# The retention gate as seven half-size products, two heads' column sums a step later, and another order in the last head's steps and in the down weights' queue

## The chip, the cores and the metric

The kernel runs on one core of a Trainium2 chip. The metric is the device time of one execution in microseconds; for the kernel before, three runs are shown, and their median is what a change is held against. One further execution was taken by the hardware profiler; every row of a profile quoted here comes from it.

Engines are named as in the profile: PE is TensorE's matmul, PEld its weight load, DVE is VectorE, ACT is ScalarE, POOL is GpSimd, SP is SyncE, which here only issues DMAs.

## The reference

One layer of a decoder trunk on a prompt of 1024 tokens and 8 sampled tokens, model width 1024. The part around the change is the hybrid mixer: one input projection whose columns are split between four heads of differential attention and four heads of retention, with a swish gate on the retention heads.

```python
z = h @ w_in                      # h = rmsnorm(x), 1032 tokens x 1024; columns: qa ka va qr kr vr gr
oa  = diff_attention(qa, ka, va)  # two softmax maps a head, with a relative bias
o_r = retention(rotary(qr), rotary(kr) * scale, vr)      # chunks of 128 tokens, state S
a = head_rms(oa) * subln * (1 - lam_init)
r = head_rms(o_r) * silu(gr)      # the gate of this change: gr is h times a 1024 x 512 slice
x = x + concat(a, r) @ w_out
x = x + cross_attention(rmsnorm(x), memory)
x = x + square(relu(rmsnorm(x) @ w_up)) @ w_down         # hidden width 4096
```

All of it is in float32. A matrix product is done as three products of rounded halves (high by high, high by low, low by high), which the names `UH`, `UL` (activations) and `wh`, `wl` (weights) stand for.

## The kernel before, in words

**Stages.** (1) Queries and keys of retention, plain products. (2) Values of attention (`va`) and then of retention (`vr`): each 1024 x 1024 x 512 product is done by `token_block` as seven products of half size (512 x 512 x 256) with sums and differences of the operand's quarters, which stand ready in `XT`; the results are put together on DVE and ACT in four `acc` tiles. (3) Retention: a loop over eight chunks of 128 tokens. A chunk `t` does four transposes of queries and keys (`tr`), the scores (`sc`), the new state (`st`), the output (`op`, from the masked scores `Sm` and the state `S`), a norm for each head times the gate (`head_norm_gate`, which yields between the sums and the scaling), and four transposes of the result into an operand of the output projection (`to_operand`: `trR`, then `rh` on ACT, `rl` on DVE and two DMAs from POOL). Between these stand the 24 products of the gate for that chunk (`tokproj_parts`, tile `grp`) as plain products of 512 columns, three pieces of 9, 12 and 3 (`SEG` and the rest). (4) Attention: four heads, ten steps each, `g` from -4 to 39; beside each step's own work, products of the next head's queries and keys (`head_proj`, tile `qkp`) are put in as filler, `FILL` at a time; in the last head the filler is work for the output projection (`pr_half`) and the sampled tokens (`dsc`), in the order that `PLAN` has. `NORM_AT` says in which steps a finished head's column sums (`ct`), its factors and their row (`hrT`) are done. (5) Output projection, cross attention, the MLP's up product and then its down product (`dn`), the last two again as seven half-size products.

**What sets the order.** Tiles are placed by a pool allocator; a scheduler orders the instructions of each engine, except where `pin` keeps PE in the order of the program, and where `issue_after` and `behind` hold an instruction back behind another one. Each engine and each DMA queue then runs its instructions strictly in that order. SP issues nearly all loads, POOL issues the operand's stores. The down product's operands are loaded by SP too: `right_lower` fetches pieces `raw_h` of the hidden rows through a ring of three `raw` buffers, `load_left` the weights `raw_d` of a quarter `g`.

## Time and profile before

| | |
|---|---|
| three runs | 1474.23, 1470.69, 1475.36 us; median 1474.23 |
| the profiled execution | 1475.19 us, its span 1473.4 us |
| busy | PE 1455.7 us (99%), DVE 1107.9 (75%), ACT 679.7 (46%), POOL 314.4 (21%) |
| granted clock | 0.996 of full speed over the span |

The span starts with the first instruction; 1.8 us of the execution lie around it. A busy PE is one with a matmul in flight: matmuls are pipelined, one of 256 columns shows some 281 ns and the next starts 119 ns later, so that costs are read from the distance of starts. Groups of instructions are given as busy time and mean length; `[2.38 <-DVE c L2546]` behind a row says how long the engine had been idle before it and what ended that.

### The profile page before, as it was taken

To read this page: it belongs to the slowest core of one execution; us is meant where nothing else is said; L and a number is where in the kernel's file an instruction comes from. 1 tells how busy PE (TensorE), PEld (TensorE's weight loads), DVE (VectorE), ACT (ScalarE), POOL (GpSimd) and SP (SyncE) were. 2 spreads that over 40 slices of the span, in tenths; PEclk is the share of its full clock that TensorE was granted. 3 is DMA by queue.
4 is the path that set the end of the run, shared out by engine and by line. 5 is a ranking of instruction groups with operands and counts; after the bars stand their busy time and mean duration, and the time that the engine had idled before them with its cause. 6 is when DMAs were issued, how large, how long until landed. Compare 5 with 4: busy or idle time off the path is not lost.

```text
span 1473.4 us, 28129 instructions
## 1 busy us (share of the span) xinstructions
PE 1455.7 (99%) x11013; PEld 1401.0 (95%) x11013; DVE 1107.9 (75%) x2263; ACT 679.7 (46%) x1327; POOL 314.4 (21%) x345
## 2 busy tenths in 40 slices
PE   9999999999999999999999999999999999999998
PEld 7899779999889999999999999999999999999998
DVE  7666536888867756567868988888888878787876
ACT  7434435666552441267436533343435443343454
POOL 0035433122304511224122000000002211110380
PEclk9999999999999999999999999999999999999998
DMA  8155738215957265654762444333446764536273
GB/s 295 62 188 171 205 70 192 72 34 159 283 169 269 100 209 170 177 178 122 236 234 77 151 159 158 138 136 133 149 159 216 262 213 144 173 105 200 71 130 116
DMA packets 129833, 238.98 MB, mean 162 GB/s; under 512 B 13606, under 2 KB 80987, under 8 KB 129572
## 3 DMA queue, kind: packets, MB, share of 16 engines
q1 hardware_dynamic: 91354, 170.66, 36.0%
q0 software_dynamic: 27472, 46.93, 11.8%
q10 hardware_dynamic: 10874, 19.60, 3.5%
q8 instruction: 86, 1.41, 0.4%
q14 instruction: 47, 0.39, 0.1%
HBM read 171.13 MB, written 58.92 MB: 156 GB/s over the span
## 4 chain that ended last, share of the span: by engine, by line
PE 88%; DVE 5%; DMA 2%; ACT 2%; issue 1%; POOL 0%; ACTq 0%; SPq 0%; DVEq 0%
PE dn L2412 20%; PE Z L2244 9%; PE qkp L75 6%; PE Y L2244 6%; PE X L2244 6%; PE mq L75 6%; PE pr_m L75 6%; PE pr_o L75 5%; PE grp L75 3%; PE sp L75 2%; PE mv L75 2%; PE mk L75 1%; PE av L75 1%; PE mpv L75 1%; PE vap_z L524 1%; PE vrp_z L524 1%
## 5 line engine op out<-in xcount | busy, mean ns | idle before, releaser
L2412 PE MATMUL dn<-UH,wd 128*128 128x258 f32 (+1 forms) x1800 | 326.6, 283 | 3.0 <-DVE c L2546 3.0
L2412 PEld LDWEIGHTS dn<-UH,wd 128*128 128x128 f32 x1800 | 279.6, 190 | 3.6 <-ACT wd L2388 2.6
L2412 PE MATMUL dn<-UL,wd 128*128 128x258 f32 x900 | 254.6, 283 | 0.0
L2412 PEld LDWEIGHTS dn<-UL,wd 128*128 128x128 f32 x900 | 170.5, 189 | 0.1
L2546 DVE TENSOR_TENSOR c<-c,dn 128x258 f32<-128x258 f32 (+1 forms) x217 | 89.1, 417 | 38.5 <-PE dn L2412 35.8
L2270 ACT ACTIVATE hq<-r 128x258 f32<-128x258 f32 x128 | 53.7, 421 | 117.4 <-DVE r L2269 117.3
L2244 PE MATMUL Z<-T_h,wu 128*128 128x258 f32 x512 | 98.1, 283 | 0.0
L2244 PE MATMUL X<-UH,wu 128*128 128x258 f32 x512 | 97.5, 282 | 0.0
L2388 ACT CAST wd<-raw_d 128x512 fp32r<-128x512 f32 x96 | 58.7, 619 | 82.0 <-PE dn L2412 77.3
L2052 ACT CAST wu<-raw_up 128x512 fp32r<-128x512 f32 x96 | 59.0, 616 | 61.0 <-PE Z L2244 52.6
L2381 ACT CAST UH<-raw_h 128x1032 fp32r<-128x1032 f32 x56 | 58.7, 1055 | 55.2 <-PE dn L2412 27.9
L2244 PEld LDWEIGHTS X<-UH,wu 128*128 128x128 f32 x512 | 81.3, 188 | 0.0
L2244 PEld LDWEIGHTS Z<-T_h,wu 128*128 128x128 f32 x512 | 81.3, 189 | 0.0
L2382 DVE TENSOR_TENSOR UL<-raw_h,UH 128x1032 fp32r<-128x1032 f32 x56 | 72.9, 1301 | 9.9 <-ACT UH L2381 9.9
L2389 DVE TENSOR_TENSOR wd<-raw_d,wd 128x512 fp32r<-128x512 f32 x96 | 72.3, 759 | 10.2 <-ACT wd L2388 10.2
L2281 POOL DMA_DIRECT2D HT<-ht x32 | 17.2, 536 | 292.1 <-DVE ht L2280 291.6
L2244 PE MATMUL Z<-T_l,wu 128*128 128x258 f32 x256 | 72.3, 282 | 0.0
L2244 PE MATMUL X<-UL,wu 128*128 128x258 f32 x256 | 72.3, 282 | 0.0
L129 ACT CAST wh_u<-raw_u 128x1024 fp32r<-128x1024 f32 x43 | 44.7, 1047 | 57.6 <-PE mq L75 39.9
L2053 DVE TENSOR_TENSOR wu<-raw_up,wu 128x512 fp32r<-128x512 f32 x96 | 64.8, 689 | 3.6 <-ACT wu L2052 3.6
L2402 POOL TENSOR_TENSOR raw_d<-raw_d,raw_d 128x512 f32<-128x512 f32 x16 | 22.1, 1384 | 197.0 <-DVE raw_d L2398 145.3
L130 DVE TENSOR_TENSOR wl_u<-raw_u,wh_u 128x1024 fp32r<-128x1024 f32 x39 | 48.6, 1257 | 20.2 <-ACT wh_u L129 20.0
(616 smaller groups left out, 4707.4 us busy)
## 6 DMA issues: line engine op xcount, KB each, us to landing
raw_u<-in_wall SPq DMA_DIRECT2D x49, 512.0 KB
HT<-ht POOLq DMA_DIRECT2D x32, 516.0 KB, 3.0
raw_h<-HT SPq DMA_DIRECT2D x32, 516.0 KB
raw_up<-in_wall SPq DMA_DIRECT2D x32, 512.0 KB
raw_d<-in_wall SPq DMA_DIRECT2D x32, 512.0 KB
HQ<-hq ACTq DMA_DIRECT2D x32, 387.0 KB
raw_h<-HQ SPq DMA_DIRECT2D x24, 516.0 KB
cmk<-in_cmk SPq DMA_DIRECT2D x16, 512.0 KB
```

What stands on the lines that cost most here:

```text
L75: pinned(nc.tensor.matmul(out, l, r, start=start, stop=stop))
L130: (lo_engine or nc.vector).tensor_sub(wl[:, :n], raw[:, :n], wh[:, :n].bitcast(F32))
L2052: nc.scalar.copy(w[:, :512], src)
L2053: nc.vector.tensor_sub(w[:, 512:], src, w[:, :512].bitcast(F32))
L2244: pinned(nc.tensor.matmul(ps, l, r[:, k, :], start=first and k == 0 and x == 0, stop=k == 3 and x == 2, skip_group_check=True))
L2270: nc.scalar.activation(h[:, PLACE[quad], :], r, AF.Square)
L2381: nc.scalar.copy(h, rv)
L2382: nc.vector.tensor_sub(l, rv, h.bitcast(F32))
L2388: nc.scalar.copy(w[:, :512], src)
L2389: nc.vector.tensor_sub(w[:, 512:], src, w[:, :512].bitcast(F32))
L2412: pinned(nc.tensor.matmul(ps[:, part], l, r[:, k, cq], start=first and k == 0 and x == 0, stop=k == 3 and x == 2, skip_group_check=True))
L2546: nc.vector.tensor_add(y, y, ps)
```

## The change

- The gate is no longer a plain product inside the retention loop. It gets a `token_block` of its own (`ga`) between `va` and `vr`, with the swish in place of the plain scaling by the row factor. Its result goes to a DRAM buffer `gated` (issued from ACT's queue), and `fetch_gate` brings 128 rows of it back for each chunk (SP's queue). The rotations of queries and keys that stood in the `vr` block stand in the `ga` block.
- In the retention loop the filler is now the first 96 of the 144 products of head 0's queries and keys, 8 ahead of the loop and 6 and 5 in each chunk (`RFILL`). The transposes of chunk `t+1` are done in chunk `t` (`turn_step`), the scaling by the gate of chunk `t-1` after them, and `trR` of chunk `t-1` behind the output of chunk `t`.
- Behind the loop the operands of head 0 are split in two pieces of 344 columns where they were one of 688, with 36 fill products left ahead of the first scores.
- `NORM_AT` for the first two heads is moved by one step, `PLAN` of the last head has two `pr_half` steps earlier, the loading of a head's values and weights stands a step off, and the four loads of down weights of quarter 1 are held back until behind the last loads of quarter 0.

On PE the retention loop has no `grp` rows any more; chunk 1 is now 2 `sc`, 4 `st`, 4 `tr`, 6 `qkp`, 8 `op`, 4 `trR`, 5 `qkp`. On DVE, chunk 0's end and chunk 1 stood like this (`Sm`: masked scores, `S`: state, `gate`: the scaled output, `sn`: state of the sampled tokens, `UL`: a piece of the activations that is restored, `s`: the heads' sums):

```order
L768 COPY S_1630<-st_1608 128x128 x2
L146 SCALAR_TENSOR_TENSOR UL<-xagain_1560,g_mix,UH 128x512 x2
L140 TENSOR_SCALAR s_0_1643<-s_0_1643 128x4
L730 COPY kT_1672<-tr_1665 128x256
L665 SCALAR_TENSOR_TENSOR gate_1641<-op_1625,r_0_1644,gate_1641 128x128 x4
L741 TENSOR_TENSOR Sm_1687<-sc_1684,maskM 128x512
L770 SCALAR_TENSOR_TENSOR S_1726<-S_1630,rdec,st_1689 128x128 x2
```

and now:

```order
L140 TENSOR_SCALAR s_0_2105<-s_0_2105 128x4
L794 TENSOR_TENSOR Sm_2123<-sc_2120,maskM 128x512
L817 SCALAR_TENSOR_TENSOR S_2160<-S_2097,rdec,st_2125 128x128
L146 SCALAR_TENSOR_TENSOR UL<-xagain_2022,g_mix,UH 128x512 x2
L767 COPY kT_2137<-tr_2130 128x256
L704 SCALAR_TENSOR_TENSOR gate_2045<-op_2092,r_0_2106,gate_2045 128x128 x4
L644 TENSOR_TENSOR kraw_2056<-qkp_1_0_2058,rb 128x344
L817 SCALAR_TENSOR_TENSOR S_2160<-S_2097,rdec,st_2125 128x128
L715 TENSOR_TENSOR rl_2169<-trR_2163,rh_2168 128x512
L140 TENSOR_SCALAR s_1_2179<-s_1_2179 128x4
L747 SCALAR_TENSOR_TENSOR sn_2190<-so_2039,rdec,vb_2041 128x512 x2
L794 TENSOR_TENSOR Sm_2204<-sc_2201,maskM 128x512
```

The scaling by the gate of chunk 0 has moved behind the restored pieces, an eviction of the filler (`kraw`) has come in, and chunk 2's `Sm` stands behind the sampled tokens' `sn`. On POOL (`r`: the heads' factors, `vb`: products for the sampled tokens, `OPH`, `OPL`: the operand's stores) the same place was

```order
L141 TENSOR_TENSOR r_0_1644<-s_0_1643,half 128x4
L703 TENSOR_TENSOR vb_1661<-vb_1661,qkd 128x1024
L678 DMA OPH<-rh_1699 128x4x128
L678 DMA OPL<-rl_1700 128x4x128
L141 TENSOR_TENSOR r_1_1739<-s_1_1738,half 128x4
```

and is now

```order
L743 TENSOR_TENSOR vb_2041<-vb_2041,qkd 128x1024
L141 TENSOR_TENSOR r_0_2106<-s_0_2105,half 128x4
L717 DMA OPH<-rh_2168 128x4x128
L717 DMA OPL<-rl_2169 128x4x128
L141 TENSOR_TENSOR r_1_2180<-s_1_2179,half 128x4
L752 DMA out_state_s<-sn_2190 128x1024
```

so that the first `vb` stands ahead of the first `r`. On SP, in the down product's quarter 0, the loads from the seventh on stood as

```order
L2375 DMA raw_h_7_2_13922<-HT 128x4x258
L2361 DMA c_13488<-X_73 128x4x516
L2492 DMA raw_d_1_1_14439<-in_wall 128x1024
L2375 DMA raw_h_4_0_13927<-HT 128x4x258
...
L2375 DMA raw_h_5_2_14180<-HT 128x4x258
L2492 DMA raw_d_0_0_14436<-in_wall 128x1024
L2492 DMA raw_d_1_0_14438<-in_wall 128x1024
L2375 DMA raw_h_3_0_14184<-HQ 128x4x258
L2492 DMA raw_d_2_0_14440<-in_wall 128x1024
L2375 DMA raw_h_3_2_14188<-HQ 128x4x258
L2361 DMA c_13489<-X_73 128x516 x4
```

and now the weights of quarter 1 come last:

```order
L2379 DMA raw_h_7_2_14121<-HT 128x4x258
L2365 DMA c_13687<-X_73 128x4x516
L2379 DMA raw_h_4_0_14126<-HT 128x4x258
...
L2379 DMA raw_h_5_2_14379<-HT 128x4x258
L2379 DMA raw_h_3_0_14383<-HQ 128x4x258
L2379 DMA raw_h_3_2_14387<-HQ 128x4x258
L2365 DMA c_13688<-X_73 128x516 x4
L2496 DMA raw_d_0_0_14635<-in_wall 128x1024
L2496 DMA raw_d_0_1_14636<-in_wall 128x1024
```

Four weight loads that stood ahead of or between `raw_h_4` to `raw_h_3` now follow them.

The diff, cut to its core:

```diff
+    gated = dram.tile([T, 512], F32, tag="gated", name="gated")
...
-        def token_block(ready, nm, out_dec, fetch, between, after):
+        def token_block(ready, nm, out_dec, fetch, between, after, func=AF.Copy):
...
-                nc.scalar.activation(y[:, cs], y[:, cs], AF.Copy, scale=rstd1[:, t : t + 1])
+                nc.scalar.activation(y[:, cs], y[:, cs], func, scale=rstd1[:, t : t + 1])
...
+        def after_ga(q, acc):
+            if q in rot_ga:
+                rotate(rot_ga[q])
+            for t in {5: range(4), 3: range(4, 8)}.get(q, ()):
+                nc.scalar.dma_start(gated[t * P : t * P + P, :], acc[t // 2][:, t % 2, :])
...
-        op_vr = token_operands(U_TOK + 4, "vr")
-        token_block(op_va, "va", vdec[:8], rot_va, after_va, op_vr)
+        op_ga, op_vr = token_operands(U_TOK + 8, "ga"), token_operands(U_TOK + 4, "vr")
+        token_block(op_va, "va", vdec[:8], rot_va, after_va, op_ga)
+        token_block(op_ga, "ga", ga8[:8], rot_ga, after_ga, op_vr, AF.Silu)
...
+        filler = head_proj(0)
+        dec = decode_step(0)
+        next(dec)
+        gate = fetch_gate(0)
+        turned = turn_step(0)
+        fill(RFILL[0])
         for t in range(8):
+            qb, kT = turned
...
-            if pend:
-                pend()
-            for _ in range(SEG[1]):
-                next(grp)
+            if t < 7:
+                turned = turn_step(t + 1)
+            if scaled:
+                with behind("DVE"):
+                    next(scaled)
+            fill(RFILL[1])
...
-            nc.scalar.activation(gate, ps, AF.Silu, scale=rstd1[:, t : t + 1])
+            if pend:
+                pend()
+            fill(RFILL[2])
             scaled = head_norm_gate(op, gate, P, t, gate)
             next(scaled)
-            if t != 5:
-                next(scaled)
+            if t < 7:
+                gate = fetch_gate(t + 1)
...
-        fill(36)
-        to_operand(gate, P, 7, "7", ("ah", "al", 2))
-        until(0, 1, 0)
         load_stacks(0)
-        for _ in load_part(0, EARLY):
-            pass
+        for c in range(2):
+            for _ in load_part(0, slice(c * CH, c * CH + CH)):
+                pass
         filler = chain(filler, rest())
+        fill(28)
+        to_operand(gate, P, 7, "7", ("ah", "al", 2))
+        fill(6)
+        to_operand(lasts[0], 8, 8, "d", ("ah", "al", 2))
...
-            load_left((0, 1) if g == 0 else range(4))
+            with tc.issue_after(seen["SP"]) if g == 1 else nullcontext():
+                load_left((0, 1) if g == 0 else range(4))
...
-PLAN = ('dhh', 'ddhhd', 'hhdhhd', 'hhdhhd', 'hhdh', 'hhdh', 'hhd', 'hh', 'hh', '', '', '')
+PLAN = ('dhh', 'dhdhdhh', 'dhhd', 'hhdhhd', 'hhdh', 'hhdh', 'hhd', 'hh', 'hh', '', '', '')
-START = 36
+START = 2
-NORM_AT = (2, 3, 4, 5, 8), (2, 5, 6, 8, 9)
+NORM_AT = (2, 4, 5, 6, 8), (2, 5, 6, 8, 9)
-SEG = (3, 4, 0)
+RFILL = (8, 6, 5)
```

More of the change, by code (lines that the diff above doesn't have):

```diff
@@ L629, in decoder_step, with fill, until @@
+        def fill(n):
+            for _ in range(n):
+                next(filler, None)
+        def until(*key):
+            while key not in done:
+                next(filler)
         pin[0] = True
-        op_vr = token_operands(U_TOK + 4, "vr")
-        token_block(op_va, "va", vdec[:8], rot_va, after_va, op_vr)
+        op_ga, op_vr = token_operands(U_TOK + 8, "ga"), token_operands(U_TOK + 4, "vr")
+        token_block(op_va, "va", vdec[:8], rot_va, after_va, op_ga)
+        ga8 = A.tile([P, 512], F32, tag="t1", name="ga_8", bufs=1)
@@ L715, in decode_step, with turn_step @@
             yield
[L717 to L722 removed]
+        def turn_step(t):
+            tr = PS.tile([P, 512], F32, tag="tr", name=f"tr_{t}", bufs=2)
             for b in range(4):
@@ L771, in decoder_step @@
             S = Sn
+            if t == 5:
+                opd = PS.tile([P, 512], F32, tag="acc", name="opd", bufs=2)
+                for g in range(4):
+                    mm(opd[32 * g : 32 * g + 32, :], hsel, wvs[g // 2][:, 4 * (g % 2) : 4 * (g % 2) + 4, :], True, True)
+            if pend:
+                pend()
+            fill(RFILL[2])
+            scaled = head_norm_gate(op, gate, P, t, gate)
+            next(scaled)
+            pend = lambda gate=gate, t=t: to_operand(gate, P, t, f"{t}", ("rh", "rl", 1))
+            if t < 7:
+                gate = fetch_gate(t + 1)
             if t < 4:
@@ L1271, in rest @@
                 yield from head_proj(h)
-        filler = head_proj(0)
         decode = decode_steps()
-        def fill(n):
-            for _ in range(n):
-                next(filler, None)
-        def until(*key):
-            while key not in done:
-                next(filler)
-        pin[0] = True
-        fill(36)
-        to_operand(gate, P, 7, "7", ("ah", "al", 2))
-        until(0, 1, 0)
-        with behind("Activation", "DVE"):
-            head_units(1)
-        load_stacks(0)
-        for _ in load_part(0, EARLY):
-            pass
-        filler = chain(filler, rest())
+        pin[0] = True
+        load_stacks(0)
+        for c in range(2):
+            for _ in load_part(0, slice(c * CH, c * CH + CH)):
+                pass
+        with behind("Activation"):
+            nc.scalar.activation(A.tile([P, 1], F32, tag="pre", name="pre"), half[:, 0:1], AF.Exp)
+        filler = chain(filler, rest())
+        fill(28)
+        to_operand(gate, P, 7, "7", ("ah", "al", 2))
+        fill(6)
+        to_operand(lasts[0], 8, 8, "d", ("ah", "al", 2))
         par = operand_steps()
@@ L1372, in decoder_step @@
             if g >= 0:
-                if x == 0:
+                if x == 0 and h:
                     load_values(h)
-                    if h < 2:
+                if x == 1 and h < 2:
+                    with tc.issue_after(seen["ACT"]):
                         head_units(h + 2)
+            if g == -1:
+                with tc.issue_after(seen["ACT"]):
+                    load_values(0)
             if h < 3:
```

211 lines of the change are left out of this document (91 added, 120 removed).

## The prediction

> **What bounds the kernel now.** I read the page first, then PE's waits, then the chain of waits, then windows by stage. The page (engines' busy time and share; below it the shares of the chain that ended last):
>
> ```profile
> PE 1455.7 (99%) x11013; PEld 1401.0 (95%) x11013; DVE 1107.9 (75%) x2263; ACT 679.7 (46%) x1327; POOL 314.4 (21%) x345
> ...
> PE 88%; DVE 5%; DMA 2%; ACT 2%; issue 1%; POOL 0%; ACTq 0%; SPq 0%; DVEq 0%
> ```
>
> PE is the bound; only two things can shorten this: less PE work, or fewer of its stops. Its stops (who waited for whom: us in total, times, longest):
>
> ```profile
> PE dn L2412 <- DVE c L2546: 3.0, 2, 2.4
> PE trA L78 <- DVE e L1034: 2.1, 2, 1.4
> PE sp L75 <- DVE mn L1019: 1.8, 2, 1.0
> ...
> PE pr_half L75 <- DVE x_half L1356: 0.6, 1, 0.6
> ...
> PE hrT L78 <- DVE c L1086: 0.3, 1, 0.3
> PE vrp_x L524 <- ACT vr L532: 0.2, 1, 0.2
> ```
>
> The largest single stop, 2.4 us, lies in the down product; `trA`, `sp`, `pr_half` and `hrT` (4.8 us) lie in attention, where DVE is nearly full. Three windows (length, then busy us of PE, PEld, DVE, ACT, POOL, the granted clock, the DMA engines' share, GB/s): retention, what follows it, and the first head.
>
> ```profile
> 144.20:232.00 87.80, 87.60 (x517) 68.68 (x515) 40.86 (x103) 36.64 (x119) 31.13 (x33) 1.00 0.54 135
> 232.00:245.00 13.00, 12.92 (x84) 12.90 (x84) 5.11 (x13) 5.46 (x8) 6.38 (x9) 1.00 0.86 178
> 245.00:300.00 55.00, 54.15 (x363) 52.98 (x362) 49.59 (x131) 35.36 (x79) 7.64 (x20) 1.00 0.42 107
> ```
>
> In retention DVE works 47% of the time, then for 13 us 39%, then 90%: the gate's 512-column products are a wide cover for a thin chain. The change takes that cover away.
>
> **The change part by part.** *The products.* Rows of the chain (start, length, what):
>
> ```profile
> 106.04 5.97 PE vrp_x L524 x48
> 112.95 17.15 PE vrp_z L524 x144
> ...
> 157.87 2.78 PE grp L75 x12
> ...
> 173.12 3.71 PE grp L286 x16
> ...
> 234.68 9.44 PE qkp L75 x60
> ```
>
> A `grp` product of 512 columns costs 2.78/12 = 231.7 ns. There are 8 chunks x 24 = 192, or 44.5 us, and the sampled tokens' 16 in 3.71: 48.2 us go. The new block is the `vr` block's copy: 7 x 2 x 2 x 4 x 3 = 336 products of 256 columns at 17.15/144 = 119.1 ns, 40.0 us, and 4 x 4 x 2 = 32 small ones (the eight between the two rows above took 112.95 - 112.01 = 0.94, so 117 ns), 3.8. So 43.8 us come: **-4.4 us**. Its sums on DVE and ACT lie under its own products, as those of `va` and `vr` do. The 96 `qkp` products in the loop are moved, not added.
>
> One more change of blocks is added. The first eviction of a block needs the `acc` tile that the last block's stores still read; `vr` paid 0.2 us for it. Between nothing and twice this row: **+0.3**.
>
> *The down weights' queue.* The timeline around the 2.4 us stop (start, length, engine, line; in brackets the idle time before), two rows of the chain, and the clock's window:
>
> ```profile
> 1170.42 0.97 SPq L2492 DMA_DIRECT2D raw_d<-in_wall  x2
> 1174.51 0.38 SPq L2375 DMA_DIRECT2D raw_h<-HQ  x1
> 1174.93 0.51 SPq L2492 DMA_DIRECT2D raw_d<-in_wall  x1
> 1177.60 0.38 SPq L2375 DMA_DIRECT2D raw_h<-HQ  x1
> ...
> 1182.78 1.06 ACT L2381 CAST UH<-raw_h 128x1032 fp32r<-128x1032 f32 x1 [5.95 <-DMA raw_h<-HQ]
> ...
> 1186.55 1.23 DVE L2382 TENSOR_TENSOR UL<-raw_h,UH 128x1032 fp32r<-128x1032 f32 x1 [0.18 <-ACT UH L2381]
> ...
> 1188.26 0.36 PE L2412 MATMUL dn<-UH,wd 128*128 128x258 f32 x1 [2.38 <-DVE c L2546]
> ```
> ```profile
> 1163.76 3.88 DMA raw_h<-HT
> ...
> 1177.60 7.84 DMA raw_h<-HQ
> ```
> ```profile
> 1189.15:1192.56 3.41, 3.41 (x18) 3.41 (x17) 2.10 (x5) 0.00 (x0) 0.00 (x0) 0.50 1.05 378
> ```
>
> Two hidden pieces asked behind three weight loads take 1182.78 - 1174.51 = 8.3 and 7.84 us, where one asked alone took 3.88. So DVE reaches their split at 1186.55, the bank's eviction stands behind it, and PE stops for 2.38 us, then runs 3.41 us at half clock, worth 1.7. Without the three loads (1.57 MB, at this window's 378 GB/s 4.2 us) the pieces land some 4 us sooner and the split ends near 1183.6, 2 us ahead of PE. The held loads then follow at about 1180; their quarter starts only after 7 x 4 x 2 groups of 12 products, beyond 1210, so nothing is late next. From -4.1 (stop and slow clock) to 0 (the stop is only moved): **-4.0**.
>
> [...]
>
> *The retention steps.* Groups of that window (busy us, mean ns) and the order of a step:
>
> ```profile
> L741 DVE TENSOR_TENSOR Sm<-sc,maskM 128x512 f32<-128x512 f32 x8 | 5.5, 684 | 3.4 <-PE sc L75 3.4
> L676 DVE TENSOR_TENSOR rl<-trR,rh 128x512 fp32r<-128x512 f32 x7 | 4.8, 688 | 2.0 <-ACT rh L675 1.1 <-DMA OPL<-rl 0.9
> L770 DVE SCALAR_TENSOR_TENSOR S<-S,rdec,st 128x128 f32<-128x128 f32 x14 | 4.2, 340 | 0.0
> ...
> L730 DVE COPY kT<-tr 128x256 f32<-128x256 f32 x8 | 3.4, 423 | 2.1 <-ACT qblk L728 2.1
> L707 DVE SCALAR_TENSOR_TENSOR sn<-so,rdec,vb 128x512 f32<-128x512 f32 x4 | 3.0, 746 | 0.0
> L146 DVE SCALAR_TENSOR_TENSOR UL<-xagain,g_mix,UH 128x512 fp32r<-128x512 f32 x4 | 2.8, 749 | 0.7 <-ACT UH L145 0.7
> ```
> ```profile
> 156.03 1.13 DVE L665 SCALAR_TENSOR_TENSOR gate<-op,r,gate 128x128 f32<-128x128 f32 x4 [0.58 <-POOL r L141]
> ```
> ```profile
> L703 POOL TENSOR_TENSOR vb<-vb,qkd 128x1024 f32<-128x1024 f32 x2 | 3.8, 1887 | 0.0
> ```
>
> The window without `grp` (48.2) and without its 24 `qkp` at 9.44/60 = 157 ns (3.8) leaves 35.8 us for eight chunks, 4.5 each; with 11 fill products (1.7) a chunk lasts 6.2 us where it lasted 10. DVE's work in a chunk: `Sm` 0.7, `kT` 0.4, four `gate` 1.1, two `S` 0.7, `rl` 0.7 and small ones 0.2, 3.8 us; chunks 1 to 3 add 1.5 for two `UL` or two `sn`, and two of them 0.5 for the filler's eviction: up to 5.8 of 6.2. I laid out chunks 0 to 3 by hand from these lengths in the new order: in chunk 1 the two `UL`, `kT` and `gate` end about 1.0 us after PE wants `trR`; in chunk 2 `Sm`, behind two `sn`, is 0.2 late; in chunk 3 `gate` 0.9; in chunk 4 `Sm` 0.3; in chunk 6 `Sm`, behind a weight split, 1.0: 3.4 in all, each stop giving the next chunk slack. From 0.5 (the first chunk alone) to 8 (the rival below): **+2.5**.
>
> *Into the first head.* Behind the loop PE has 33 `qkp`, `trR`, 8 `qkp`, about 7.7 us, until the first scores. DVE must finish chunk 7 (`rl`, `gate` and an eviction behind `r`, some 5 us), then split the keys, and POOL must send eight copies, where the 13 us window above had DVE and POOL half free. From 0 to 3: **+1.0**.
>
> *Attention.* The column sums a step later free `hrT`'s 0.3; two `pr_half` steps earlier put 0.9 us of PE work ahead of scores that waited for DVE. Where DVE is the one that is late, moving filler moves the stop; from -4 (of the 4.8 nearly all gone) to +2: **-1.0**.
>
> Sum: -4.4 + 0.3 - 4.0 + 2.5 + 1.0 - 1.0 = **-5.6 us**. Against the profiled execution's own 1475.19 us this gives 1469.6; that execution lies 1 us above the median of 1474.23, so I say **1469.5**.
>
> **The rivals.** *All covered:* stops give slack, and DVE's 40.9 us, less what goes with `grp`, fit under some 51; then only the two savings stay, with -1 in attention: 1475.2 - 4.4 + 0.3 - 4.0 - 1.0 = 1466. For it: no engine but DVE is over 90% in a chunk. Against it: every engine runs in order, and the late ones stand ahead of the wanted ones.
>
> *The cover's loss eats the saving:* retention costs 5 and the head's start 3 instead of 2.5 and 1: 1474. For it the 90% of DVE in the window from 245; against it that there PE still lost only 0.85 us in 55.
>
> *The down product's stop stays or moves:* +4: 1473.5. Against it the margin of 2 us.
>
> *Slower:* the retention window's loads (size of each):
>
> ```profile
> brep<-brow SPq DMA_DIRECT2D x1, 2304.0 KB
> ...
> vb<-vrd SPq DMA_DIRECT2D x4, 256.0 KB
> xagain<-in_xT SPq DMA_DIRECT2D x2, 512.0 KB
> ```
>
> On POOL the first `vb` (1.9 us) now stands ahead of the first `r`, and it needs two of these loads, the second asked behind both `xagain`; `gate`, then `trR`, wait for that `r`. If they land some 11 us into the loop, PE stops 4.5 us in chunk 1, and in chunk 3, where two `vb` stand ahead of `r`, 2.4 more, each followed by 1.7 us of slow clock: +10.3 for the 2.5, 1477.5. It decides from a landing later than 7 us into the loop; with the head's start at 3 as well, 1479.5. For it: the DMA engines' share, 0.86 in the window behind retention; against it that `brep`, the largest load of this loop, now stands in the `vr` block.
>
> [...]
>
> That the change doesn't do what it says is excluded by the order: 208 `grp` products are gone, 368 of the block are there.
>
> **How the numbers follow.** My case 45% (1467 to 1472.5), all covered 22%, saving eaten 13%, stop stays 9%, slower 11%. A change is told from none here from 0.3%, 4.4 us: below 1469.8 is faster, above 1478.7 slower. Half of my case and nearly all of the covered one are faster: 0.48 with a little of the others; half of the slower case ends above 1478.7, with some room for what I haven't seen 0.09; the rest, 0.43, is the same. The range goes from 1463 (covered, attention at -4) to 1477, which leaves out most of the slower case.
>
> **What would show it.** `gap` rows in place of `grp`, some 44 us long; PE's start of retention 44 us later and its loop some 52 to 54 us long; PE waiting in it for `gate`, `Sm` or `r`, up to 1 us at a time; no half clock near the down product's start, and `raw_h` landing in 4 us there. Wrong: a PE stop over 2.4 us in retention, `vb` as what `r` waits for, a new wait for `raw_d`, or waits in attention that grew by more than 2 us.

## The result, and the profile after

| | before | changed |
|---|---|---|
| runs | 1472.90 us median of 8 (1470.58 to 1475.36) | 1482.01 us median of 8 (1477.90 to 1482.88) |
| profiled execution, its span | 1475.19, 1473.4 us | 1482.29, 1480.5 us |

The changed kernel is slower: 1.0052 of the time before, interval 1.0041 to 1.0063, where 1469.5 us, 0.3% less than the 1474.23 of the kernel before, was forecast and 1477 was the upper end of the range. Its runs fall into two groups, three at 1478 to 1479 and five at 1482 to 1483; what parts them is the clock, below.

The page after the change (engines' busy time; shares of the chain that ended last) and PE's waits (who waited for whom: us in total, times, longest):

```profile
PE 1458.4 (99%) x11173; PEld 1410.6 (95%) x11173; DVE 1123.6 (76%) x2284; ACT 684.2 (46%) x1341; POOL 317.7 (21%) x349
...
PE 83%; DVE 7%; DMA 3%; issue 2%; ACT 2%; POOL 1%; SPq 0%; DVEq 0%; ACTq 0%; POOLq 0%
```
```profile
PE sp L75 <- DVE mn L1025: 4.6, 6, 2.8
PE trA L78 <- DVE e L1040: 3.0, 4, 1.6
PE av L75 <- DVE al L1059: 1.4, 1, 1.4
...
PE dn L2416 <- DVE c L2551: 0.9, 2, 0.6
```

The stop in the down product is gone (3.0 to 0.9 us), but `sp`, `trA` and `av`, all in attention, now wait 9.0 us where they waited 4.2 (0.3 of it `av`). To see where the time went, the program was cut at the same instructions in both traces: the first product of the added or the `vr` block, the first transpose of retention (the sampled tokens' `tr_d`), the first score, the last half product, and the first product of `mq` (cross attention), of the up and of the down product. Windows (length, then busy us of PE, PEld, DVE, ACT, POOL, the granted clock, the DMA engines' share, GB/s), first before, then after; the after has one row more, for the added block:

```profile
99.00:143.30 44.30, 44.08 (x371) 43.14 (x369) 30.28 (x36) 17.71 (x26) 26.73 (x17) 1.00 0.56 191
143.30:249.60 106.30, 106.01 (x638) 87.06 (x638) 51.06 (x119) 43.62 (x130) 37.51 (x42) 1.00 0.61 144
249.60:444.70 195.10, 189.92 (x1375) 179.97 (x1375) 159.18 (x426) 116.64 (x250) 40.47 (x75) 1.00 0.51 147
...
1133.80:1473.40 339.60, 330.54 (x2742) 329.60 (x2740) 268.36 (x445) 146.13 (x242) 79.95 (x74) 0.98 0.53 159
```
```profile
99.40:143.10 43.70, 43.70 (x370) 43.16 (x369) 31.42 (x36) 16.01 (x24) 26.12 (x16) 1.00 0.59 196
143.10:186.80 43.70, 43.70 (x370) 43.06 (x368) 21.05 (x23) 15.64 (x24) 1.31 (x3) 1.00 0.45 153
186.80:245.00 58.20, 57.53 (x429) 50.53 (x429) 41.78 (x108) 31.85 (x116) 32.10 (x34) 1.00 0.86 201
245.00:453.50 208.50, 197.91 (x1376) 183.92 (x1375) 164.84 (x436) 117.55 (x254) 47.15 (x87) 0.98 0.53 144
...
1144.00:1480.50 336.50, 329.73 (x2742) 328.56 (x2740) 269.30 (x445) 146.40 (x242) 79.84 (x74) 0.99 0.54 160
```

The two blocks take 87.4 us for 44.3 (+43.1). Retention up to the first score takes 58.2 for 106.3 (-48.1), for the same PE work less the 208 `grp` products. Together that is **-5.0**, all that the products could give. Then attention, with the same PE work (1376 matmul records for 1375), takes 208.5 for 195.1: **+13.4**. The down product gives -3.1, the stages between them +1.4, the start +0.4; the sum is the 7.1 us between the spans. So the question is attention. Cut at every 48th of its 192 score products: 39.7, 44.1, 44.9, 34.1 us (to the last of them) and a rest of 32.4 us before; 43.8, 49.4, 47.0, 36.5 and 31.8 after.

The largest of its stops is this one; the timeline after (start, length, engine, line; in brackets the idle time before and what ended it):

```profile
388.04 0.27 PE L78 MATMUL hrT<-ident,c 128*8 128x128 f32 x1 [0.23 <-DVE c L1106]
...
391.93 0.33 SPq L1116 DMA_DIRECT2D rbh<-hrow  x1
...
398.10 1.29 DVE L1143 TENSOR_TENSOR oraw<-oraw,rbh 128x512 f32<-128x512 f32 x2 [1.89 <-DMA rbh<-hrow]
...
400.12 0.41 PE L75 MATMUL sp<-KA,Q 128*128 128x320 f32 x1 [2.77 <-DVE mn L1025]
```

and this is the same place before:

```profile
376.44 0.27 PE L78 MATMUL hrT<-ident,c 128*8 128x128 f32 x1
...
379.96 0.32 SPq L1110 DMA_DIRECT2D rbh<-hrow  x1
...
385.80 0.69 DVE L1137 TENSOR_TENSOR oraw<-oraw,rbh 128x512 f32<-128x512 f32 x1 [0.47 <-DMA rbh<-hrow]
```

A finished head's factors go through `hrT` to DRAM and come back as a row over all partitions, `rbh`, 9.4 us later before (376.44 to 385.80) and 10.1 us later after (388.04 to 398.10). `NORM_AT` moved the sums, the factors and `hrT` by a step, but not its last entry, the step in which DVE multiplies by the row (8 in both). DVE reaches that instruction, waits 1.89 us for the row, and the score evictions behind it wait too; PE stops for 2.77 us. The row is made in two DMAs on SP's queue: the second, `rbh`, is asked 3.5 us (before) and 3.9 us (after) behind `hrT` and lands 5.8 and 6.2 us later.

The second place, after the change and, in the second block, before:

```profile
326.86 0.39 PE L75 MATMUL av<-al,VH 128*128 128x256 f32 x1 [1.38 <-DVE al L1059]
...
328.36 2.97 PE L75 MATMUL ct<-ones,sq 128*128 128x1 f32 x16
```
```profile
322.74 1.84 PE L75 MATMUL ct<-ones,sq 128*128 128x1 f32 x16
```

Before, the 16 records of `ct` stood ahead of that weighing (`av`), and PE had them to do while DVE made `al`. They now come behind it. The windows there, and behind the 2.77 us stop:

```profile
325.42:328.83 3.41, 2.03 (x16) 1.97 (x16) 3.32 (x5) 1.25 (x2) 0.31 (x2) 1.00 0.32 61
328.83:332.24 3.41, 3.41 (x17) 3.41 (x17) 0.85 (x5) 0.00 (x0) 0.42 (x1) 0.50 0.00 0
332.24:335.66 3.42, 3.42 (x16) 3.36 (x15) 0.69 (x1) 0.58 (x1) 1.24 (x1) 0.50 0.00 0
...
400.51:403.93 3.42, 3.42 (x27) 2.71 (x25) 3.42 (x12) 1.15 (x4) 0.00 (x0) 0.50 1.18 389
```

Each stop is followed by half clock, 6.83 and 3.41 us of it. There `av` products of 256 columns start 213 or 214 ns apart, 120 just ahead of it, and the records of `ct` 213 for 112: some 4.6 us lost, by an estimate from these distances. In the second window PE is busy all the time, with `ct`, and yet a third one at half clock follows.

### The profile page after: what moved, and what is told of

Same layout as the page of the kernel before. It is cut to its first block, busy times and chain, and to the rows that moved or that the text cites. A ratio compares the mean times of both kernels' runs of the same rounds, so it can differ in the third digit from the quotient of the medians.

```text
span 1480.5 us, 28578 instructions
## 1 busy us (share of the span) xinstructions
PE 1458.4 (99%) x11173; PEld 1410.6 (95%) x11173; DVE 1123.6 (76%) x2284; ACT 684.2 (46%) x1341; POOL 317.7 (21%) x349
## 4 chain that ended last, share of the span: by engine, by line
PE 83%; DVE 7%; DMA 3%; issue 2%; ACT 2%; POOL 1%; SPq 0%; DVEq 0%; ACTq 0%; POOLq 0%
PE dn L2416 20%; PE Z L2248 9%; PE Y L2248 6%; PE mq L75 6%; PE pr_m L75 6%; PE X L2248 6%; PE qkp L75 5%; PE pr_o L75 2%; PE mv L75 2%; PE mk L75 1%; PE av L75 1%; PE mpv L75 1%; PE vap_z L507 1%; PE gap_z L507 1%; PE vrp_z L507 1%
## 5 line engine op out<-in xcount | busy, mean ns | idle before, releaser
L2393 DVE TENSOR_TENSOR wd<-raw_d,wd 128x512 fp32r<-128x512 f32 x96 | 70.2, 738 | 10.8 <-ACT wd L2392 10.7
L1031 ACT ACTIVATE e<-e,mn 128x128 f32<-128x128 f32 (+6 forms) x64 | 49.7, 777 | 33.0 <-DVE mn L1025 32.4
L75 PE MATMUL qkp<-UH,wh_u 128*128 128x344 f32 x192 | 63.8, 332 | 0.3 <-DVE gate L704 0.3
```

Of the source, the lines that this page charges most:

```text
L75: pinned(nc.tensor.matmul(out, l, r, start=start, stop=stop))
L1031: nc.scalar.activation(e[:, :n], e[:, :n], AF.Exp, bias=mn[:, m : m + 1], scale=-1.0, accum_out=sm[:, m, q : q + 1])
L2393: nc.vector.tensor_sub(w[:, 512:], src, w[:, :512].bitcast(F32))
```

## The experiments

Medians in us; the ratio is to the runs of the kernel before on the same chip (their medians 1473.65, 1473.84, 1473.59 and 1473.88 in the four groups). "Lost to the clock" is the mean span times one less the mean granted clock; the last column is the mean span without it. That takes half clock for half the pace, where by the distances above it is 1.8 to 1.9 times as slow, so that the loss is a little high. In all 17 profiles the last 4.7 to 9.1 us of the span are at half clock, while PE's last product ends 5.7 to 6.1 us before the span does: 2.4 to 4.6 us of what each of these executions "lost" lie there, most of it with no product left to slow, so that only differences between the rows count.

| run | median (runs) | ratio and interval | lost to the clock | rest |
|---|---|---|---|---|
| before (all its runs of the first two groups) | 1473.8 (46) | | 4.6 | 1467.6 |
| changed | 1482.0 (8) | 1.0052 (1.0041 to 1.0063) | 6.7 | 1472.4 |
| a_norm: sums as before | 1479.8 (5) | 1.0035 (1.0021 to 1.0049) | 7.1 | 1470.3 |
| a_plan: last head's order as before | 1480.8 (5) | 1.0056 (1.0042 to 1.0069) | 8.3 | 1471.5 |
| a_out9: the row's reader a step later too | 1480.7 (5) | 1.0048 (1.0034 to 1.0062) | 6.8 | 1472.2 |
| b_norm: before, sums a step later | 1477.6 (10) | 1.0025 (1.0016 to 1.0035) | 7.1 | 1468.9 |
| b_down: before, down weights held back | 1474.1 (12) | 1.0006 (0.9997 to 1.0014) | 4.5 | 1468.1 |
| n_nodown: sums as before, weights not held | 1478.1 (8) | 1.0026 (1.0016 to 1.0036) | 6.6 | 1469.5 |
| n_rfill: sums as before, 16 fill moved | 1476.0 (11) | 1.0018 (1.0009 to 1.0026) | 5.8 | 1468.5 |
| n_ct: sums as before, `ct` in pairs | 1478.8 (11) | 1.0029 (1.0016 to 1.0042) | 5.8 | 1471.0 |
| b_ct3: before, `ct` three times | 1488.9 (4) | 1.0103 (1.0089 to 1.0118) | 11.9 | 1474.9 |
| n_rfill2: sums as before, 32 fill moved | 1481.6 (5) | 1.0056 (1.0043 to 1.0069) | 10.4 | 1468.7 |
| n_vals: n_rfill, values loaded as before | 1478.8 (6) | 1.0035 (1.0022 to 1.0048) | 6.9 | 1470.7 |
| n_rfill2v: both of the last two | 1482.0 (6) | 1.0052 (1.0040 to 1.0064) | 6.9 | 1473.0 |
| a_rfill: changed, 16 fill moved | 1479.4 (6) | 1.0048 (1.0034 to 1.0063) | 7.1 | 1470.8 |
| n_plan: n_rfill, last head's order as before | 1476.1 (11) | 1.0016 (1.0006 to 1.0026) | 5.9 | 1468.5 |
| n_chunk: n_plan, 24 fill moved | 1476.8 (11) | 1.0022 (1.0011 to 1.0033) | 5.6 | 1469.4 |

### The column sums a step later

```diff
 # a_norm: the changed kernel; b_norm makes the opposite edit in the kernel before
-NORM_AT = (2, 4, 5, 6, 8), (2, 5, 6, 8, 9)
+NORM_AT = (2, 3, 4, 5, 8), (2, 5, 6, 8, 9)
```

> The changed kernel with only the column-sum steps put back (NORM_AT's first row 2, 3, 4, 5, 8 as before; all else as changed). Theory A: the sums a step later cost about 8 us in attention in two ways. The eight ct products of head 0 no longer stand ahead of the weighing that waits for al (a PE stop of 1.38 us near 326, then 6.83 us at half clock), and the gain row leaves one step later while its reader (oraw<-oraw,rbh on DVE) stays, so DVE waits for the row (0.61 us near 349, 1.89 us near 396) with score evictions queued behind it (PE stops of 1.6 and 2.77 us, then 3.41 us at half clock). Then this run takes 7 to 9 us less than the changed kernel, about 1474, the span's clock is 0.997 or more, and the three places show no PE stop over 1 us. Rival B: DVE carries work into attention that the thinner retention no longer hides, and stops wherever it is full; then this run gains at most 2 us and the stops only move.

> The kernel before with only the column sums a step later (NORM_AT's first row 2, 4, 5, 6, 8). Theory A: it is slower than the kernel before by 5 to 9 us though retention is untouched, with a PE stop at al<-trA near 329 us and a DVE wait for rbh near 394 us. Rival B (the thinner retention is the cause): within 1.5 us of the kernel before.

In the kernel before, where nothing else was touched, the edit costs 3.7 us (2.4 to 5.2; theory A had 5 to 9). Its trace has the predicted wait, and the stop, in the kernel with the old retention:

```profile
393.51 1.29 DVE L1137 TENSOR_TENSOR oraw<-oraw,rbh 128x512 f32<-128x512 f32 x2 [2.30 <-DMA rbh<-hrow]
...
395.53 0.63 PE L75 MATMUL sp<-KA,Q 128*128 128x320 f32 x1 [3.09 <-DVE mn L1019]
```

followed by 6.83 us at half clock. The stop at `al` did not come in it. In the changed kernel, undoing the edit takes the stop at `al` away and brings the other two down to 0.73 and 0.87 us, but gains only 2.2 us, not 7 to 9, and the intervals of the two versions overlap: a stop of 0.64 us at `ct`, which waits for `sq` on ACT, comes in place of the one at `al`, and that profile has half clock there too and at two more places. So theory A has the mechanism right and about doubles its size; rival B as put (at most 2 us, stops only move) is excluded by b_norm, though about half of the loss is left for it.

```diff
 # a_out9: the changed kernel
-NORM_AT = (2, 4, 5, 6, 8), (2, 5, 6, 8, 9)
+NORM_AT = (2, 4, 5, 6, 9), (2, 5, 6, 8, 9)
```

> The changed kernel with the reader of the gain row a step later as well (NORM_AT's first row 2, 4, 5, 6, 9 in place of 2, 4, 5, 6, 8). Theory A: DVE no longer waits for the row, so the stops near 355 and 397 us (1.6 and 2.77 us) and the half clock behind the second go, some 4 to 5 us; the stop near 326 us stays, since the ct products are still late there. Rival B (DVE is simply full): no gain over 1 us. Rival C (the order in the last head): the stop near 397 us stays.

DVE now waits 0.57 us for the row instead of 1.89, but the two products by `rbh` then stand ahead of another thing that PE wants:

```profile
393.75 0.69 DVE L1143 TENSOR_TENSOR oraw<-oraw,rbh 128x512 f32<-128x512 f32 x1 [0.57 <-DMA rbh<-hrow]
...
399.44 0.42 PE L75 MATMUL pr_half<-UH,wh_u 128*128 128x344 f32 x1 [3.62 <-DVE x_half L1354]
```

The stop moved and grew, and the median stayed within 1.3 us. Not all of the 3.62 us is the row's: one product `e` in front of that eviction takes 1.80 us, where 0.75 is usual (below, the cover of the first head). The expectation of 4 to 5 us is missed: the place of the waits changed and their sum did not fall, 10.2 us of PE's stops in attention as changed and 10.8 here.

### The last head's order

```diff
 # a_plan: the changed kernel
-PLAN = ('dhh', 'dhdhdhh', 'dhhd', 'hhdhhd', 'hhdh', 'hhdh', 'hhd', 'hh', 'hh', '', '', '')
+PLAN = ('dhh', 'ddhhd', 'hhdhhd', 'hhdhhd', 'hhdh', 'hhdh', 'hhd', 'hh', 'hh', '', '', '')
```

> The changed kernel with only the last head's order put back (PLAN as before; all else as changed). Theory A (the sums a step later are the cause): the time stays within 1.5 us of the changed kernel, and the stops near 326, 355 and 397 us stay. Rival C (the other order of the decode and half steps costs the time after 384 us): 2 to 3 us less than the changed kernel, and the 2.77 us stop near 397 goes.

1.2 us less, with five runs spread over 3.4 us; the stops of 1.40, 1.60 and 2.54 us stay where they were. n_plan, with eleven runs beside n_rfill's eleven (below), has 1476.1 against 1476.0, and 1468.5 in both without the loss to the clock. Rival C's 2 to 3 us are out; whatever the order is worth lies within some 2 us of nothing. (n_plan's stretch from score 144 to the last half product is 2.7 us longer than n_rfill's, where 0.5 was allowed; two half-clock windows, 3.4 us, fall into it.)

### The down weights' queue

```diff
 # b_down: the kernel before; n_nodown undoes it in a_norm
-            load_left((0, 1) if g == 0 else range(4))
+            with tc.issue_after(seen["SP"]) if g == 1 else nullcontext():
+                load_left((0, 1) if g == 0 else range(4))
```

> The kernel before with only the down weights' loads held back (the one line at load_left; all else as before). As predicted, the 2.38 us stop and the half clock at the down product's start are gone, raw_h lands in about 4 us, and the time falls by 3 to 4 us. Rival: the stop is not there in every execution (the run with only the sums moved, which has the old queue, showed 0.61 us there and no half clock), so the median falls by 1 us or less.

> The changed kernel with the column sums as before and the down weights' loads not held back. As predicted for the queue: a PE stop of 2.4 us and a half clock return at the down product's start, and the time is 3 to 4 us above the run with the sums as before. Rival (the stop comes only in some executions): within 1.5 us of it.

Nothing: 1.0006 (0.9997 to 1.0014), that is from 0.4 us less to 2.1 more, and n_nodown is not slower than a_norm. Not that the edit fails: with it `raw_h` is not asked behind `raw_d`, and the wait for it is shorter (b_down: asked at 1175.92, split begun at 1181.02). But the old queue does not always make PE stop that long. In b_norm, which has it:

```profile
1182.30 0.38 SPq L2375 DMA_DIRECT2D raw_h<-HQ  x1
...
1188.76 1.05 ACT L2381 CAST UH<-raw_h 128x1032 fp32r<-128x1032 f32 x1 [4.04 <-DMA raw_h<-HQ]
```

6.5 us from the request to the split (6.2 in n_nodown) where the profile before had 8.3, with the same order on the queue. PE's stops there are 0.60 us, and 0.42 in n_nodown. In b_ct3 (below), the fourth profile with the old queue, the split begins 6.4 us after the request and PE stops for 1.29 us. Half clock follows only in the profile before. So 1.1 us or more of the 2.38 us stop, and its half clock, are what that one execution had; what made its load land 2 us later than the same request in the other three is open. The edit is not free of stops either: b_down's profile has two of 0.66 and 0.58 us, at 1203.9 and 1211.9.

### The cover of the first head

```diff
 # n_rfill: a_norm with 16 qkp out of the loop (a_rfill: the same two edits in the changed kernel)
-RFILL = (8, 6, 5)
+RFILL = (8, 5, 4)
...
         load_stacks(0)
+        fill(16)
         for c in range(2):
```

> The changed kernel with the column sums as before and 16 of the first head's qkp moved out of the retention loop (RFILL 8, 5, 4 in place of 8, 6, 5), to stand between the loop and the first key splits. Theory D: the first head is slow (43.8 us from the first score to the 49th against 39.7 before) because DVE comes out of the loop with chunk 7's work and the key splits in hand; 2.5 us more of pure PE work there let it catch up, so that stretch shrinks by 1.5 to 2.5 us while the loop, which has hardly a stop, does not grow by it. Rival E: the loop was just covered; it then stops 2 us more, and nothing is gained.

> The changed kernel with only 16 qkp moved from the retention loop to before the first key splits; the column sums stay a step later. So far: changed 1482.0, with the sums as before 1478.1 to 1479.8, with both 1476.0. If the parts add, this run is at 1478.5 to 1480, its first stretch at 42.0 us, and the DVE wait for rbh near 394 us and the PE stop behind it stay. If the sums a step later cost nothing by themselves and all was carried DVE work, it is at 1476 like the run with both.

As theory D has it: the stretch of the first 48 scores falls from 43.8 to 42.0 us, and the loop stays (58.2 us from its first transpose to the first score, a_norm 57.7). The run is the best of the changed family, 1476.0. With a_rfill the four corners are 1482.0 as changed, 1479.4 with the fill moved, 1478.1 to 1479.8 with the sums as before, 1476.0 with both: the parts add within a microsecond, though with five to eleven runs each no such difference is known to better than some 2 us. The first two rows are that stretch before and as changed; the two behind them are from n_rfill, the loop and the stretch:

```profile
249.60:289.30 39.70, 38.85 (x258) 37.80 (x258) 36.03 (x99) 26.82 (x58) 5.39 (x14) 1.00 0.38 106
```
```profile
245.00:288.80 43.80, 41.11 (x258) 37.49 (x257) 39.90 (x109) 27.24 (x62) 13.67 (x25) 1.00 0.55 126
```
```profile
187.00:245.10 58.10, 57.63 (x429) 50.37 (x430) 43.14 (x112) 32.02 (x116) 33.91 (x37) 1.00 0.89 206
245.10:287.10 42.00, 40.10 (x258) 37.56 (x258) 38.09 (x105) 27.29 (x62) 11.90 (x22) 1.00 0.56 124
```

PE has the same 258 products in each. What differs is DVE's work: 36.03 us in 39.7 before, 39.90 in 43.8 as changed, 38.09 in 42.0 here, 37.52 in 40.9 in n_rfill2. It is 91 or 92% of the stretch in these four, and DVE's idle time stays between 3.4 and 3.9 us: the stretch grows and shrinks by what DVE's work does. What came ahead of the first score before is now done here. By their lengths (which overlap a little) the splits of keys and queries are 2.05 us of it, `rl` of chunk 7 and of the sampled tokens 0.9, an eviction of the filler and the page table's indices 1.0.

Another 0.9 us is no carried work of DVE's. One product `e` takes 1.65 us, after, where the same one took 0.75 before:

```profile
259.06 2.99 POOL L1001 TENSOR_TENSOR VL<-vraw,VH 128x512 fp32r<-128x512 f32 x2 [4.37 <-ACT VH L999]
259.24 1.65 DVE L1040 SCALAR_TENSOR_TENSOR e<-e,mn,e 128x512 f32<-128x512 f32 x1
```
```profile
262.27 0.75 DVE L1034 SCALAR_TENSOR_TENSOR e<-e,mn,e 128x512 f32<-128x512 f32 x1
```

POOL splits the head's values (`VL`) beside it, which it had done at 239.3 us before, ahead of the first score. In all 17 profiles such an `e` of 512 columns takes 0.74 to 0.75 us when no piece of `VL` is running as it starts (36 times), and 1.31 to 1.85 us when one is or starts within 0.04 us of it (32 times); each time it then ends 0.54 to 0.55 us behind that piece. The long `e` in a_out9 is one of these, and so is the one that the 1.4 us stop at `trA` waits for in the kernel before (394.10 us, 1.81 long).

```diff
 # n_rfill2: n_rfill with 32 moved
-RFILL = (8, 5, 4)
+RFILL = (8, 4, 3)
...
-        fill(16)
+        fill(32)
```

> The changed kernel with the column sums as before and 32 qkp moved out of the retention loop (RFILL 8, 4, 3), to stand ahead of the first key splits; with 16 moved, the stretch from the first score to the 49th was 42.0 us. Theory D (DVE comes out of the loop with work in hand): that stretch falls further, to 40.5 to 41.5 us, the next 48 scores lose their stops near 313 and 322 us, and the time falls by 1 to 2 us below the run with 16 moved, unless the loop, now 5.6 us a chunk, gains stops. Rival E (the loop's cover is used up): the loop to the first score grows by as much as is gained, 1 us or more.

The stretch does fall to 40.9, but the loop grows to 60.9 us, with a stop in it of a kind that the prediction had named:

```profile
209.47 0.49 PE L75 MATMUL op<-vr,Sm 128*128 128x128 f32 x2 [2.04 <-DVE Sm L794]
```

so rival E holds from here on: between 16 and 32 the loop's cover is used up. The next 48 scores take 45.7 us, against 44.1 before: moving the fill does not lower them. The time did not fall by the expected 1 to 2 us. The median, 1481.6, is worse than that trace tells (its own execution was one of 1475.9); four of its five runs lost 10 us or more to the clock.

```diff
 # n_chunk: n_plan with 24 moved, 8 of them from chunks 4 to 7 alone
-            fill(RFILL[1])
+            fill(RFILL[1] - (t > 3))
...
-            fill(RFILL[2])
+            fill(RFILL[2] - (t > 3))
```

> The changed kernel with the sums as before, 16 qkp moved, and the last head's order (PLAN) as before too. If the order costs something, as the 1.2 us of the run with it alone undone hint, 1474 to 1475, and the PE stop of 0.86 us at sp behind pr_half near 391 us gives way to those of the kernel before (0.7 to 1.0 and 1.4 us, which would make it no better). If the order is worth nothing, 1476 within 1 us, the stretch from score 144 to the last half product unchanged within 0.5 us.

> As the last one, with 24 qkp moved, the last 8 only from chunks 4 to 7 (the 2.04 us stop at Sm with 32 moved was in the early chunks, which carry the splits and the decode step). Theory D: the loop gains no stop over 0.5 us, the first stretch falls to about 41.4 us, and the time is at or below 1475, within 1 us of the kernel before.

n_chunk has a first stretch of 41.0 us and gives it back as a loop of 60.2, with a stop of 0.70 us behind the loop: 1476.8, above the 1475 expected and no gain on n_plan. n_plan itself, in which the block, the loop with the splits behind it and the order of the loads (values, weights, down weights) are what is left of the change, stands 2.2 us above the kernel before (1.0006 to 1.0026). None of these versions beats the kernel before.

```diff
 # n_vals: n_rfill (n_rfill2v: n_rfill2)
-                if x == 0 and h:
+                if x == 0:
                     load_values(h)
...
-            if g == -1:
-                with tc.issue_after(seen["ACT"]):
-                    load_values(0)
```

> The run with 16 qkp moved, and head 0's values loaded at its first weighing step again, as before the change (VH on ACT and VL on POOL, 1.2 and 3.0 us, leave the first scores' steps). If the values' earlier load is a part of the first head's slowness, the first stretch falls from 42.0 us by 0.5 us or more; if DVE alone sets it (theory D), by less than 0.3 us, and the time stays within 1 us.

> Both together: 32 qkp moved and head 0's values loaded as before the change. By theory D as with 32 moved alone, 1474 to 1475 us. If both parts count, about 1473.5, that is no slower than the kernel before.

Both expectations are missed, to the other side: the first stretch grows to 43.5 and 44.7 us. In n_vals PE stops 2.06 us at `sp` near 260 us where n_rfill stops 0.51. The edit does not do what was expected of it: the step in the program is later, but the `issue_after` that held the split behind ACT is gone with it, and in time the split comes earlier. `VH` and `VL` begin at 256.6 to 258.6 us in n_rfill, at 243.5 to 254.8 in n_vals, at 238.6 to 240.6 before. So what the two runs show is that holding the split back is a part of the change that earns something here. DVE's work in the stretch, 38.4 us in n_vals and 38.0 in n_rfill2v, is that of n_rfill (38.1): its amount does not explain these two, and why the early place costs that much was not followed up.

### Half clock, idle time and streamed columns

Two runs with the stop of 1.4 us at `al` (a_plan, a_out9) have no half clock behind it, while a_norm has it behind 0.64 us. Through each profile a grid of 3.413 us can be laid on which all its half-clock stretches begin. For each window of the grid the columns streamed were summed (a matmul's columns times 231.7/512 = 0.45 ns, from the prediction's `grp` row).

```diff
 # n_ct: a_norm, in norm_factors, behind every second ct
+                if h < 2 and x % 2:
+                    fill(2)
+                    lent[0] += 2
 # b_ct3: the kernel before; the added columns are read by nobody
-                mm(ct[:, x : x + 1], sq[:, x * P : x * P + P], ones[:, :1], True, True)
+                for y in range(3 if h < 2 else 1):
+                    mm(ct[:, x + 16 * y : x + 16 * y + 1], sq[:, x * P : x * P + P], ones[:, :1], True, True)
```

> The changed kernel with the column sums as before, and in them the eight ct products of a head taken two by two with two qkp between (the same number of qkp is left out later). In all six profiles so far the clock's windows lie on a grid of 3.413 us, and a window in which the products' columns stream for under about 0.42 of its time is followed by one at half clock; ct streams one column in some 260 ns, so eight of them fill a window with next to nothing. Theory F: with qkp between them no window of heads 1 and 2 near 322 and 366 us falls under 0.5, and no half clock follows there; the time falls by up to 2 us and its spread over the runs shrinks. Rival: what halves the clock is PE's stops alone, and the ct products have no part in it; then a stop there is followed by half clock as often as before.

> The kernel before with each of the eight ct products of heads 0 and 1 issued three times (the second and third into columns nobody reads): 32 products, 64 matmul records of 111 ns more, 7.1 us of PE work without a wait in it, and nothing else. Theory F (the clock goes by how long columns stream in a window of 3.413 us, not by whether PE waits): 48 such records in a row, 5.3 us, leave at least one window of the grid nearly without streamed columns, so half clock follows near 326 and near 372 us in the profile though PE does not stop there, and the time rises by 7.1 us and 2 to 7 us more. Rival: only PE's idle time counts; then no half clock follows there, and the time rises by 7 us.

n_ct misses, by an error in its own sum: two `ct` products are four records of 111 ns, 0.44 us, and two `qkp` stream for 0.31, a share of 0.41, not above 0.5. Its window at 324.1 us streamed for 0.40 and was followed by half clock, with 0.10 us of idle time in it; the spread of its runs, 1474.9 to 1483.8, did not shrink. That doesn't tell the theories apart. b_ct3 does:

```profile
322.20:325.60 3.40, 3.40 (x32) 3.40 (x30) 1.53 (x3) 1.57 (x3) 1.73 (x5) 1.00 0.73 180
325.60:329.01 3.41, 3.41 (x18) 3.41 (x18) 0.00 (x0) 0.00 (x0) 0.00 (x0) 0.50 0.69 134
329.01:332.43 3.42, 3.42 (x15) 3.36 (x16) 1.78 (x6) 0.00 (x0) 1.33 (x1) 0.50 0.00 0
332.43:335.84 3.41, 3.41 (x16) 3.41 (x15) 2.71 (x6) 1.90 (x3) 1.35 (x1) 0.50 0.00 0
```

PE is busy in every window and the clock is at half for three of them, and for one more at 380.2 us. The time rises by 15.3 us, a little above the 9 to 14 expected. The time without the clock's loss rises by 7.3 us (1474.9 against 1467.6 for the same group's runs before), the 7.1 that the added products take; the loss to the clock rises by 7.6, from 4.3 to 11.9. So here half clock came without idle time in the window ahead of it (3.40 us busy of 3.40). Idle time also came without half clock: stops of 1.39 us (a_out9, 327.1) and 1.61 us (a_rfill, 351.4) lay in windows that streamed for 0.47 and 0.40 of their time, and none followed.

Over all 17 profiles, between 10 and 1462 us, with each record counted from its start for its columns times 0.45 ns and overlaps counted once: of 45 windows that streamed for less than 0.40 of their time, 36 were followed by half clock; of 46 at 0.40 to 0.47, one; of 7125 above, none. Of the nine below 0.40 without half clock behind them, two lay in half-clock stretches themselves, where products start 1.8 to 1.9 times as far apart (above), and two hold retention's `op` products, whose 128 columns start 111 ns apart where 0.45 ns a column gives 58, so that this count may be too low for them. Counted without the overlaps the figures shift by a few windows (33 of 39, 3 of 34, 1 of 7143). Whether half clock goes with few columns or with something else about such thin products (those of 1 and of 128 columns alike start 111 or 112 ns apart), no run here separates.

## Why the prediction was wrong, point by point

**What bounds the kernel** (PE, with DVE nearly full in attention): right, and the second half of it decided.

**The products, -4.4, and one more block change, +0.3**: right. The two blocks took 43.1 us more, the forecast was 44.1.

**The retention steps, +2.5, and into the first head, +1.0**: near in sum up to the 49th score (4.1 against 3.5), but by luck: wrong in place and, with what follows, too small. Up to the first score nothing was lost (-48.1 us against 48.2 of `grp`; PE's longest waits from the loop to the first score are 0.2 and 0.3 us), so the stops laid out by hand chunk by chunk, 3.4 us of them, did not come. The first 48 scores then cost 4.1 us more, with 3.9 us more of DVE's time in them. The next 48 cost another 1.6 where no half clock falls in them (45.7 in n_nodown and n_plan, 44.1 before); DVE has only 0.6 us more there, 0.6 is a wait of `ct` for `sq` that the kernel before has not, and the rest stays open. So 5.7 against 3.5; the term that was mis-sized is "into the first head: from 0 to 3". The prediction took PE's loss of 0.85 us in 55 before as a sign of room, but the windows it showed had DVE at 90% there: DVE's work is not made less by a shorter loop, it comes later, into the one stretch whose length goes with DVE's work. And beside POOL's split of the values, which came along, one `e` on DVE took 1.65 us for 0.75, 0.9 us of it; the prediction has no term for that.

**The down weights' queue, -4.0**: the first step that failed. The stop and its half clock were costed from one profiled execution and taken off a median; alone, the edit is worth 0.9 us the other way (-0.4 to +2.1). That the profiled execution lay 1 us above the median was said, but not that what raised it could be the very stop. The rival "the stop stays or moves" had 9%, and its reason was wrong too: in three other executions with the old queue the stop was 0.42 to 1.29 us, without half clock.

**Attention, -1.0**: the second step that failed, off by 3 to 5 us. "The column sums a step later free `hrT`'s 0.3" looked at what waits for the sums' inputs and not at who reads their result: the row takes 9.4 to 10.1 us through DRAM, its reader on DVE was not moved, and it had already waited 0.47 us before. And the 16 `ct` records were PE's work while DVE made `al`. By itself the edit costs 3.7 us; undone in the changed kernel it gives 2.2 (to 3.9, with n_nodown). The other half of the term, two `pr_half` steps earlier, is not told from nothing.

**The slower rival** had the wrong mechanism: `vb` on POOL did stand ahead of the first `r`, but its load landed just in time.

```profile
193.68 1.90 POOL L743 TENSOR_TENSOR vb<-vb,qkd 128x1024 f32<-128x1024 f32 x1 [24.80 <-DMA vb<-vrd]
195.74 1.04 POOL L141 TENSOR_TENSOR r<-s,half 128x4 f32<-128x4 f32 x1 [0.17 <-PE st L75]
```

At 193.7 us, 6.9 behind the loop's start at 186.8. The rival decided from 7 us, so that it did not come true by 0.1 us, which is luck (its time adds up to 1477.3, not 1477.5); there is no stop in that chunk. No run shows the 1.7 us of slow clock that it put behind each of its stops: no half clock falls between 4.6 and 328.8 us of the span after, and the stop of 2.04 us in n_rfill2's loop has none behind it (clock 1.00 from 186.6 to 288.4 us). Other stops over 2.3 us had 3.41 us of it behind them (before, 1188.3; changed, 400.1) or 6.83 (b_norm, 395.5); 3.41 us of it cost 1.5 by the distance of starts (`dn` of 258 columns, before: 214 to 218 ns in it, some 119 behind it). "The cover's loss eats the saving" (13%) was the nearest, with 1474 too low since the down product's 4 us were in it.

**The signs** named were mostly right: `gap` some 44 us long (43.7), waits for `gate` and `Sm` under 1 us, no half clock near the down product's start, `raw_h` there 3.7 us from its request to its split, and, as a sign of being wrong, waits in attention grown by more than 2 us, which they did. The loop was shorter than the 52 to 54 us named: 49.7 us from 186.8 to its last `op` at 236.5, since its stops did not come.

The sum as it came out, in medians: products and blocks up to the first score -5.0; the first 96 scores +5.7, of which 3.9 is DVE's time; sums +2 to +4; queue and last head's order 0. That is +3 to +5 of the 8 to 9 us. The rest: about 2 us is a larger loss to the clock (6.7 against 4.6), a part of which is in the terms above; +0.9 us is the up product's stage (327.1 us for 326.2), with a stop of 0.55 us some 9 us into it in most of the changed profiles, which was not looked into; and a microsecond or two stays open, as much as these medians differ by themselves.

## What to carry to other kernels

A stop that one profile shows is a price for that execution; before it is taken off a median, ask whether the runs' times agree that it is always there. When a wide cover is taken away, add up the work of the engine it covered, and look for it in the next stretch where that engine is full. See which of POOL's instructions come to lie beside DVE's there. When a producer is moved later, look at its readers' places on their in-order engines, and at what the moved work itself had been covering.

## What the runs showed of the hardware

In these 17 profiles half clock went with few streamed columns, with idle time of PE and without it. The stretches at half clock begin on a grid of 3.413 us, whose place in the span is not always the same (counted back in steps of 3.4133 us, its first line is at 1.3 us before, 1.2 as changed and 2.0 in b_norm). By the count above, windows of the grid that streamed columns for less than 0.40 of their time were mostly followed by one at half clock (36 of 45), those at 0.40 to 0.47 once (1 of 46), those above never (0 of 7125). In b_ct3, four windows are at half clock and PE is busy in each of them, and so it is in the windows ahead, at 322.2 and 376.8 us (3.40 us of 3.40), where one-column products start 111 ns apart. Of four stops of 1.38 to 1.40 us, one was followed by 6.83 us at half clock (as changed, 326.9 us), and three by none (a_plan 326.4, a_out9 327.1, the kernel before 396.0). That it depends on where the grid lies is the author's reading; no run moved the grid by itself. The changed kernel's runs, in two groups 4 us apart, had a granted clock of 0.996 to 0.998 in the one and 0.994 to 0.995 in the other, and 0.0025 of 1480 us is 3.7 us.

`e` on DVE and `VL` on POOL took longer side by side. An `e` (128x512, float32) took 1.31 to 1.85 us when a piece of `VL` was running on POOL as it started, ending 0.54 to 0.55 us behind that piece, and 0.74 to 0.75 us otherwise; a `VL` that started 0.1 to 0.4 us behind an `e` took 1.48 to 1.78 us, where the shortest took 1.26. Why is not shown, and only these two operations were looked at.

In chunk 1 of the changed kernel DVE and POOL started their instructions in the order that is listed ahead of the prediction, and so did SP in the down product's quarter 0: `Sm` at 195.51 us, `S` 196.11, `UL` 196.37, `kT` 197.69, `gate` 198.03, `kraw` 199.06 on DVE; `vb` at 193.68, `r` 195.74, `OPH` 200.70, `OPL` 201.55 on POOL; the last two `raw_h` from 1184.57, `c` from 1187.76, `raw_d` from 1189.72 on SP.
